# Where tiles begin in a partition of SBUF: two layers of a decoder trunk on one core, with operands of TensorE moved by 32 to 512 bytes

## The chip, the core and the metric

The kernel runs on one core of a Trainium2 chip. Times are device microseconds of one execution. The engines are PE (TensorE: matmuls, and PEld for the loading of their weights), DVE (VectorE), ACT (ScalarE), POOL (GpSimd) and SP, which here only issues DMAs. SBUF is the core's memory of 128 partitions; "a tile begins at byte b" means the byte within each partition. What is measured is the median time of the whole launch.

## The reference, cut to what matters

Two layers over 512 tokens of 1024 columns. Each layer adds, in this order, a half-step SwiGLU feed-forward net (FFN), a token mixer (differential attention in layer 0, causal pooling in layer 1), a cross attention with 4 heads into 256 memory tokens, and a second FFN; after each comes a layer norm. All in float32.

```
for i in range(DEPTH):                                   # DEPTH = 2
    x = layer_norm(a*x + 0.5*swiglu_ffn(x, w_in[i,0], w_out[i,0]))      # 1024 -> 2*2816 -> 1024
    h = diff_attention(x, ...) if i == 0 else pool_mixer(x, ...)
    x = layer_norm(a*x + h)
    x = layer_norm(a*x + memory_cross_attention(x, mem, wq[i], wkv[i], wo[i]))
    x = layer_norm(a*x + 0.5*swiglu_ffn(x, w_in[i,1], w_out[i,1]))
```

## The kernel before

Every float32 product is made of three matmuls: each operand is split into a rounded part (hi, made by a cast on ACT) and the rest (lo, made by a subtraction on DVE), and `mm3` issues hi·hi, hi·lo and lo·hi. So wh and wl are the two parts of a weight tile, xh and xl those of the transposed activations. A matmul names a stationary operand, 128 columns of it, loaded by an LDWEIGHTS of its own, and a moving operand of 256 or 512 columns. Which of the two a "weight" of the network is depends on the stage: in the FFN's first half and the query projections x moves and the weight is loaded; in the FFN's second half (`down`, `plain_down`) and the output projections (`to_tokens`) the weights move and the activations (ha, hb, xe, oT) are loaded.

The FFN's first half uses a seven-product scheme (`up`) with moving operands of 256 columns; 7,392 of the 13,104 matmuls stand there. Its second half has moving operands of 512 columns. The differential attention (DA) projects q and k with 512 columns, v with 256; the cross attention projects q with 512 (for some parts 256) and the memory's k and v with 256.

SBUF is laid out by pools that are opened one behind the other. `stage_pools` opens the pools of weights of a stage (wh, wl, and the raw float32 they are split from), `phase_pool` those of a phase. A tile's place follows from the order of the pools and their sizes; `pad` opens an idle pool of some bytes so that what follows begins elsewhere. `APART` is 64, `ROUND` is 512. Sizes of nearly all tiles are multiples of 512 bytes, so what a pad sets holds until the next pad. Pools of different stages lie over one another: a tile of a later stage that covers a byte of a tile of an earlier one has to wait until that one is read for the last time, whatever the number of bytes.

The output projection of DA (`to_tokens` at the end of `diff_attention`) keeps the split weights of its last half in tiles that are free by then: `low, low, p, p`. The cross attention of layer 0 begins beside it: `load_memory("p")` loads the 256 memory tokens into four tiles p (four DMAs on SP's queue, which is strictly in order), transposes them on PE (line 1175) and splits them into mem0h, mem0l and so on; `xa_kv` then splits its first weights (lines 237 and 239) and multiplies them with the memory (pk, pv). The layer norm between them works token block by token block (X_74 to X_77 are the four blocks): `ln_add` (line 352) adds the projection, `ln_token` computes the mean (361), the variance (ACT line 374, POOL lines 375 and 376) and scales (378, 380).

The order of instructions on each engine is set when the program is built, by the tile framework's scheduler, from its dependences; each engine then runs its own list strictly in order and waits at semaphores.

Of the kernel before, what the change touches and what calls it, by code (L numbers as in the profile page):

```python
# [9 lines left out]
F32 = mybir.dt.float32  # L10
# [7 lines left out]
P = 128  # L18
# [33 lines left out]
APART, ROUND, LINE = 64, 512, 480  # L52
# [52 lines left out]
class Trunk:  # L105
# [31 lines left out]
            pool = ctx.enter_context(self.pool("pad"))  # L137
            pool.tile([P, nbytes // 4], F32, tag="pad", name="pad")

    def to_x(self, ctx):  # L140

        self.pad(ctx, ROUND - APART)

    def to_w(self, ctx):

        self.pad(ctx, APART)

    @contextmanager
    def phase_pool(self, gain, spare, **bufs):

        self.gain, self.spare, self.bufs, self.phase = gain, spare, bufs, {}
        with ExitStack() as ctx:
            for t in bufs:
                if t == "_x":
                    self.to_x(ctx)
                else:
                    self.phase[t] = ctx.enter_context(self.pool(t))
            yield  # L160

    @contextmanager
    def stage_pools(self, w, raw, order):

        with ExitStack() as ctx:
            self.stage = {}
            for n in order:
                if n == "wl" and order[0] == "mem" or n == "wh" == order[0]:
                    self.to_w(ctx)
                self.stage[n] = ctx.enter_context(self.pool(n))  # L170
            self.banks = {n: ctx.enter_context(self.pool(n, space=PSUM)) for n in ("px", "py", "yz")}
            self.w_bufs, self.raw_bufs, self.aux_turn = w, raw, 0
            yield
# [982 lines left out]
    def load_memory(self, tag=None):  # L1156

        nc = self.nc
        src = self.a["mem"][0].rearrange("(m p) (h d) -> p m h d", p=P, h=2)
        if tag:  # L1160
            raw = [[self.tmp(tag) for h in range(2)] for m in range(2)]
            for m in range(2):
                for h in range(2):
                    nc.sync.dma_start(raw[m][h], src[:, m, h])
        else:
            t = self.raw_tile((2, 2, S))
            nc.sync.dma_start(t, src)
            raw = [[t[:, m, h] for h in range(2)] for m in range(2)]
        self.memT = []
        for c in range(0, KC, 2):  # L1170
            pt = self.aux("pt").rearrange("p (c m n) -> p c m n", c=2, m=2)
            for i in range(2):
                for m in range(2):
                    o = (c + i) % 4 * P
                    self.nc.tensor.transpose(pt[:, i, m], raw[m][c // 4][:, o : o + P], self.ident)
            t = tuple(self.stage["mem"].tile([P, 2, MEM], F32R, name=f"mem{c}{n}") for n in "hl")
            self.split(t[0], t[1], pt.rearrange("p c m n -> p c (m n)"))
            self.memT += [(t[0][:, i], t[1][:, i]) for i in range(2)]
        if tag and LINE < 480:
            self.stage["mem"].tile([P, (480 - LINE) // 4], F32, name="mempad")  # L1180

    def xa_kv(self, w, h):
        nc = self.nc
# [102 lines left out]
            yield from self.xa_head(*self.heads[h][1])  # L1286

    def cross_attention(self, layer, ln):
        bufs = dict(q=8, oT=10, gb=2)
        if layer == 0:  # L1290
            self.kv = []
            mem = self.side_pool("mem")
            with self.other_pools():
                self.stage["mem"] = mem
                with self.phase_pool(("gb", "gb"), "p", pT=6, p=4, kv=8, _x=0, **bufs):
                    self.kvp = self.phase["kv"]
                    with self.tc.high_priority():
                        self.load_memory("p")
                    self.xa(layer, ln)
            self.close_side()  # L1300
        else:
            with self.later, self.phase_pool(("gb", "gb"), "p", _x=0, pT=6, p=4, **bufs):
                self.xa(layer, ln)

    def xa(self, layer, ln):
# [44 lines left out]
        self.side.pop().__exit__(None, None, None)  # L1350

    def ffn_pools(self):
        return self.stage_pools(4, dict(ra=4, rc=3), ("wh", "wl", "ra", "rc"))

    def other_pools(self, order=("wh", "wl", "raw")):
        return self.stage_pools(5, dict(raw=2), order)

    def ffn_phase(self, **more):
        bufs = dict(b1=1, b3=1, b2=1, b4=1, _x=0, xe=6, hb=4, sp=4, ha=4, sr=1, hr=3)
        return self.phase_pool(("hr", "sr"), "sp", **bufs, **more)  # L1360

    def ffn_first(self, layer, ln):
# [13 lines left out]

    def mixer(self, layer, ln):
        if layer == 0:
            bufs = dict(low=4, rt=2, a=4, p=4, o=1, qk=8, _x=0, v=4, oT=11)
            with self.other_pools(), self.phase_pool(("v", "v"), "rt", **bufs):  # L1380
                self.diff_attention(layer, ln)
            self.close_side()
        else:
            self.later = ExitStack()
            self.later.enter_context(self.other_pools(("mem", "wl", "raw", "wh")))
            self.kvp = self.later.enter_context(self.pool("kv"))
            bufs = dict(pw=1, pb=2, ps=2, ones=1, _x=0, pooled=20, sq=1)
            with self.phase_pool(("pooled", "pooled"), "sq", **bufs):
                side = self.pool_mixer(layer, ln)
                with self.tc.high_priority():  # L1390
                    self.load_memory()
                next(side)
                self.kv = []
                self.weave(self.early_kv(layer, 2), side, 900, 4300)
            self.close_side()
# [45 lines left out]
```

## Time and profile before

| | |
|---|---|
| runs | median 1972.75 us of three, 1970.02 to 1975.78 |
| the profiled execution | 1976.36 us, of which the profile's span is 1974.6 us |
| PE busy | 97% of the span, 13,104 matmuls, and as many weight loads |
| DVE, ACT, POOL busy | 79%, 51%, 16% |
| granted clock of TensorE, mean | 0.995 |

Matmuls are pipelined: a row's duration is longer than the distance from one start to the next. What a stream of matmuls costs is therefore read from starts: the start of the first and of the last of a run of equal ones, divided by the number of steps between them. The view by line gives the duration of one; it goes up and down with that distance, but is not it.

### The profile page before, as it was taken

What the parts mean: (1) busy time and instruction counts of PE and PEld (TensorE: products, weight loads), DVE (VectorE), ACT (ScalarE), POOL (GpSimd) and SP (SyncE); (2) the same over time, 40 slices, a digit from 0 to 9 for tenths busy, and PEclk for the clock granted to TensorE, in tenths of its full rate; (3) what the DMA queues carried; (4) which work ended last, traced back from release to release, by engine and by line L of the source; (5) the groups of instructions that cost most, each with busy time, mean ns of one, the idle gap of its engine ahead of it and who ended that gap; (6) DMA issues with size and microseconds to landing.
All of it is one profiled execution on the core that took longest, in us unless ns stands there. A gap on an engine that the chain in (4) does not pass through costs nothing. (4 is left out here: it accounts for less than half of the span.)

```text
span 1974.6 us, 32506 instructions
## 1 busy us (share of the span) xinstructions
PE 1920.2 (97%) x13104; PEld 1749.0 (89%) x13104; DVE 1566.1 (79%) x2208; ACT 1016.0 (51%) x1545; POOL 320.1 (16%) x297
## 2 busy tenths in 40 slices
PE   7999999999999999999999999999999999999998
PEld 7999998888778888999998999999788889899996
DVE  7888987888867558789887888888777457888886
ACT  5554553466655435555553655555445435555552
POOL 1122121111211002221220311211100013111211
PEclk9999999999999999999999999999989999999999
DMA  9988772322134316977783787877254336877861
GB/s 238 197 171 181 166 156 64 89 65 86 45 116 139 108 65 160 203 176 166 145 193 112 149 176 168 181 171 139 77 171 131 104 96 143 168 173 170 184 143 46
DMA packets 246743, 277.96 MB, mean 141 GB/s; under 512 B 8256, under 2 KB 212544, under 8 KB 246592
## 3 DMA queue, kind: packets, MB, share of 16 engines
q0 software_dynamic: 92928, 92.29, 30.3%
q1 hardware_dynamic: 153664, 183.59, 28.8%
q8 instruction: 103, 1.69, 0.3%
q14 instruction: 48, 0.39, 0.1%
HBM read 273.75 MB, written 2.10 MB: 140 GB/s over the span
## 5 line engine op out<-in xcount | busy, mean ns | idle before, releaser
L578 POOL DMA_DIRECT2D ra<-in_ffn_w_in_dram x132 | 171.4, 1316 | 1017.0 <-DVE wl L115 850.9
L114 ACT CAST wh<-ra 128x1024 fp32r<-128x1024 f32 x184 | 192.9, 1053 | 218.1 <-DMA ra<-in_ffn_w_in_dram 55.7
L115 DVE TENSOR_TENSOR wl<-ra,wh 128x1024 fp32r<-128x1024 f32 x184 | 223.6, 1221 | 82.1 <-ACT wh L114 81.4
L114 ACT CAST wh<-rc 128x1024 fp32r<-128x1024 f32 x136 | 142.7, 1053 | 129.3 <-PE x L198 39.2
L197 PE MATMUL x<-xh,wh 128*128 128x256 f32 x704 | 197.5, 281 | 6.3 <-DVE hr L644 4.1
L197 PE MATMUL x<-xe,wh 128*128 128x256 f32 x704 | 195.3, 277 | 3.1 <-ACT sp L639 1.7
L198 PE MATMUL x<-xl,wh 128*128 128x256 f32 x704 | 196.5, 279 | 1.5 <-DVE xl L115 1.5
L199 PE MATMUL x<-xh,wl 128*128 128x256 f32 x704 | 196.1, 279 | 0.8 <-DVE wl L115 0.8
L198 PE MATMUL x<-xe,wh 128*128 128x256 f32 x704 | 194.8, 277 | 0.0
L199 PE MATMUL x<-xe,wl 128*128 128x256 f32 x704 | 194.7, 277 | 0.0
L115 DVE TENSOR_TENSOR wl<-rc,wh 128x1024 fp32r<-128x1024 f32 x136 | 164.6, 1220 | 27.5 <-ACT wh L114 27.1
L114 ACT CAST wh<-b 128x1024 fp32r<-128x1024 f32 x112 | 117.7, 1051 | 125.7 <-PE x L198 62.0
L115 DVE TENSOR_TENSOR wl<-b,wh 128x1024 fp32r<-128x1024 f32 x112 | 136.8, 1222 | 41.0 <-ACT wh L114 41.0
L197 PEld LDWEIGHTS x<-xh,wh 128*128 128x128 f32 x704 | 133.2, 189 | 9.4 <-issue 4.4
L197 PEld LDWEIGHTS x<-xe,wh 128*128 128x128 f32 x704 | 132.2, 188 | 5.0 <-ACT ha L639 1.9
L198 PEld LDWEIGHTS x<-xl,wh 128*128 128x128 f32 x704 | 133.4, 189 | 3.3 <-DVE xl L115 2.1
L199 PEld LDWEIGHTS x<-xh,wl 128*128 128x128 f32 x704 | 133.2, 189 | 1.0 <-DVE wl L115 1.0
L198 PEld LDWEIGHTS x<-xe,wh 128*128 128x128 f32 x704 | 132.3, 188 | 1.3
L199 PEld LDWEIGHTS x<-xe,wl 128*128 128x128 f32 x704 | 132.4, 188 | 0.0
L115 DVE TENSOR_TENSOR wl<-raw,wh 128x1024 fp32r<-128x1024 f32 x64 | 80.5, 1264 | 56.1 <-ACT wh L114 55.4
L114 ACT CAST wh<-raw 128x1024 fp32r<-128x1024 f32 x64 | 66.6, 1051 | 71.5 <-PE xq L198 22.7
L199 PE MATMUL z<-xh,wl 128*128 128x256 f32 x352 | 97.9, 280 | 4.0 <-DVE wl L115 4.0
(413 smaller groups left out, 6156.5 us busy)
## 6 DMA issues: line engine op xcount, KB each, us to landing
ra<-in_ffn_w_in_dram POOLq DMA_DIRECT2D x132, 512.0 KB, 7.2
rc<-in_ffn_w_in_dram SPq DMA_DIRECT2D x88, 512.0 KB, 6.0
b<-in_ffn_w_out_dram SPq DMA_DIRECT2D x76, 512.0 KB, 5.7
ra<-in_ffn_w_in_dram SPq DMA_DIRECT2D x44, 512.0 KB, 4.7
rc<-in_ffn_w_in_dram POOLq DMA_DIRECT2D x44, 512.0 KB, 9.8
raw<-in_xa_wkv_dram SPq DMA_DIRECT2D x16, 1024.0 KB, 5.3
raw<-in_da_w_qkv_dram SPq DMA_DIRECT2D x16, 512.0 KB, 5.2
raw<-in_xa_wq_dram SPq DMA_DIRECT2D x8, 1024.0 KB, 5.1
```

Of the source, the lines that this page charges most:

```text
L114: self.nc.scalar.copy(hi, src),
L115: self.nc.vector.tensor_sub(lo, src, hi.bitcast(F32)),
L197: mm(out, w[0], x[0], start=start, stop=False, skip_group_check=again)
L198: mm(out, w[0], x[1], start=False, stop=False, skip_group_check=again)
L199: self.last_mm = mm(out, w[1], x[0], start=False, stop=stop, skip_group_check=again)
L578: nc.gpsimd.dma_start(t, source(*block), accum_op=ALU.add)
```

## The change

The two functions that padded at fixed places give way to one, `step`, and a list of pools can name a pad wherever it likes: `_off` is 64 bytes, `_32` and `_96` are 32 and 96, any other (`_on`, `_on_gb`) is 448. The pads are then set anew in each stage. No operation, no tile and no size is added or removed apart from the pads, and the strip at the end of the memory's pool.

```
+    def step(self, ctx, name):
+        given = {"_off": APART, "_32": 32, "_96": 96}
+        self.pad(ctx, given.get(name, ROUND - APART))
...
-                if n == "wl" and order[0] == "mem" or n == "wh" == order[0]:
-                    self.to_w(ctx)
-                self.stage[n] = ctx.enter_context(self.pool(n))
+                if n[0] == "_":
+                    self.step(ctx, n)
+                else:
+                    self.stage[n] = ctx.enter_context(self.pool(n))
...
-        if tag and LINE < 480:
-            self.stage["mem"].tile([P, (480 - LINE) // 4], F32, name="mempad")
+        if tag:
+            self.stage["mem"].tile([P, (ROUND - APART) // 4], F32, name="strip")
...
-        bufs = dict(q=8, oT=10, gb=2)
+        bufs = dict(_off=0, q=8, _on=0, oT=10, _on_gb=0, gb=2)
...
-            with self.other_pools():
+            with self.other_pools(("_32", "wh", "wl", "raw")):
...
-                with self.phase_pool(("gb", "gb"), "p", pT=6, p=4, kv=8, _x=0, **bufs):
+                with self.phase_pool(("gb", "gb"), "p", pT=6, p=4, kv=8, **bufs):
...
-            with self.later, self.phase_pool(("gb", "gb"), "p", _x=0, pT=6, p=4, **bufs):
+            with self.later, self.phase_pool(("gb", "gb"), "p", pT=6, p=4, **bufs):
...
-        return self.stage_pools(4, dict(ra=4, rc=3), ("wh", "wl", "ra", "rc"))
+        return self.stage_pools(4, dict(ra=4, rc=3), ("_off", "wh", "wl", "ra", "rc"))
...
-        bufs = dict(b1=1, b3=1, b2=1, b4=1, _x=0, xe=6, hb=4, sp=4, ha=4, sr=1, hr=3)
+        bufs = dict(b1=1, b3=1, b2=1, b4=1, _on=0, xe=6, _off=0, hb=4, sp=4, ha=4, sr=1, hr=3)
...
-            bufs = dict(low=4, rt=2, a=4, p=4, o=1, qk=8, _x=0, v=4, oT=11)
+            bufs = dict(low=4, rt=2, a=4, p=4, o=1, qk=8, v=4, oT=11)
...
-            self.later.enter_context(self.other_pools(("mem", "wl", "raw", "wh")))
+            self.later.enter_context(self.other_pools(("mem", "_96", "wl", "raw", "wh")))
...
-            bufs = dict(pw=1, pb=2, ps=2, ones=1, _x=0, pooled=20, sq=1)
+            bufs = dict(pw=1, pb=2, ps=2, ones=1, _off=0, pooled=20, sq=1)
```

Where tiles begin, as the remainder of their first byte by 512, before and after:

| stage | tiles | before | after |
|---|---|---|---|
| all | xh, xl | 480 | 480 |
| FFN | wh, wl / xe / ha, hb | 32 / 480 / 480 | 32 / 480 / 32 |
| DA | wh, wl, low, a, p, qk / v, oT | 32 / 480 | 480 / 480 |
| cross attention, layer 0 | wh, wl, pT, p, kv / mem / q / oT | 32 / 480 / 480 / 480 | 0 / 32 / 64 / 0 |
| pooling and cross attention, layer 1 | wh, wl, kv / pT, p / mem / q / oT | 32 / 480 / 480 / 480 / 480 | 64 / 64 / 480 / 128 / 64 |

While a matmul streams its moving operand, PE loads the weights of the next one. The *distance* in what follows is the start of a matmul's moving operand less the start of the next matmul's weights, by 512, written between -255 and 256. Counted over the list of matmuls, float32 ones that are followed by another such:

| columns | distance before | after | matmuls |
|---|---|---|---|
| 256 | -64 | -64 | 7,272 |
| 256 | 64 | 0 / -64 / -32 / 96 | 354 / 266 / 189 / 188 |
| 256 | -64 | -96 / 32 / 0 | 279 / 187 / 80 |
| 512 | 64 | 0 | 1,667 |
| 512 | -64 | 0 | 406 |
| 512 | 0 | 64 | 376 |
| 512 | -64 | -32 / -96 | 189 / 139 |
| 512 | 64 | 64 | 289 |
| 512 | 0 | 0 | 195 |

One more thing follows from the places. Before, the stages DA and cross attention of layer 0 begin with the same pad, and the four tiles p of the cross attention lie exactly on the four tiles a of DA (bytes 137,760 to 145,952). After, DA has no pad and the cross attention one of 32 bytes: DA's a lies at 137,696 to 145,888 and its p from 145,888 on; the cross attention's p at 137,728 to 145,920, so that the last of them covers 32 bytes of DA's first p.

The order of instructions is the same on every engine except at this one boundary, on DVE, ACT, PE and SP (and two loads for a layer norm of layer 1 that change places on SP). On DVE, before, from the addition for the third token block's end to the third weight split (X_76 and X_77 are the last two token blocks, mem0l to mem6l the low parts of the transposed memory, wl those of the first weights of `xa_kv`):

```order
L352 SCALAR_TENSOR_TENSOR X_77,sums<-X_77,ps 128x512
L378 SCALAR_TENSOR_TENSOR X_76<-X_76,mean,v 128x1024
L115 TENSOR_TENSOR mem4l<-pt,mem4h 128x512
L380 SCALAR_TENSOR_TENSOR X_76<-X_76,rstd,v 128x1024
L115 TENSOR_TENSOR xl<-pt,xh 128x4x128 x2
L352 SCALAR_TENSOR_TENSOR X_77,sums<-X_77,ps 128x512
L115 TENSOR_TENSOR mem0l<-pt,mem0h 128x512
L115 TENSOR_TENSOR mem2l<-pt,mem2h 128x512
L115 TENSOR_TENSOR mem6l<-pt,mem6h 128x512
L361 TENSOR_SCALAR mean<-sums 128x1
L239 TENSOR_TENSOR wl<-raw,wh 128x1024
```

And the same place of the change (its line numbers are two lower):

```order
L350 SCALAR_TENSOR_TENSOR X_77,sums<-X_77,ps 128x512
L376 SCALAR_TENSOR_TENSOR X_76<-X_76,mean,v 128x1024
L115 TENSOR_TENSOR xl<-pt,xh 128x4x128
L378 SCALAR_TENSOR_TENSOR X_76<-X_76,rstd,v 128x1024
L115 TENSOR_TENSOR xl<-pt,xh 128x4x128
L350 SCALAR_TENSOR_TENSOR X_77,sums<-X_77,ps 128x512
L359 TENSOR_SCALAR mean<-sums 128x1
L376 SCALAR_TENSOR_TENSOR X_77<-X_77,mean,v 128x1024
L378 SCALAR_TENSOR_TENSOR X_77<-X_77,rstd,v 128x1024
L237 TENSOR_TENSOR wl<-raw,wh 128x1024 x2
L115 TENSOR_TENSOR mem0l<-pt,mem0h 128x512
```

The whole scaling of the last token block and two weight splits now stand ahead of mem0l, where before mem0l followed the addition at once. On ACT, in the same way, the last block's square (`rt,var<-X_77,mean`) now stands ahead of the casts of wh and mem0h. On PE, before, from the last two products of DA's output projection on:

```order
L199 MATMUL ps<-p,oT 128x512
L1175 MATMUL pt<-ident,p 128x128 x12
L197 MATMUL pk<-mem0h,wh 128x256
L197 MATMUL pv<-wh,mem0h 128x256
L198 MATMUL pk<-mem0l,wh 128x256
```

And of the change:

```order
L197 MATMUL ps<-p,oT 128x512
L1173 MATMUL pt<-ident,p 128x128 x16
L195 MATMUL pk<-mem0h,wh 128x256
L196 MATMUL pk<-mem0l,wh 128x256
```

All sixteen transposes of the memory now stand behind the projection, where four of them stood within it, and the product with mem0l is PE's second one after them. On SP the four loads of p stand where they stood, but the second of them now waits for a product of DA's output projection that reads p, and the loads behind it in SP's queue wait with it.

More of the change, by code (lines that the diff above doesn't have):

```diff
@@ L138, in pad @@
             pool.tile([P, nbytes // 4], F32, tag="pad", name="pad")
[L140 to L146, printed above, removed]
+    def step(self, ctx, name):
+        given = {"_off": APART, "_32": 32, "_96": 96}
+        self.pad(ctx, given.get(name, ROUND - APART))
     @contextmanager
@@ L155, in phase_pool @@
             for t in bufs:
-                if t == "_x":
-                    self.to_x(ctx)
+                if t[0] == "_":
+                    self.step(ctx, t)
                 else:
```

## The prediction

> **What bounds the kernel now.** I read the page first, then the order of time on PE.
>
> ```profile
> span 1974.6 us, 32506 instructions
> PE 1920.2 (97%) x13104; PEld 1749.0 (89%) x13104; DVE 1566.1 (79%) x2208; ACT 1016.0 (51%) x1545; POOL 320.1 (16%) x297
> ```
>
> PE is busy for 97% of the span, so the time is the sum of the distances between matmul starts, plus the few places where PE stands. The change touches both: how fast a stream of matmuls runs, and one place where PE may stand. For the first, the timeline of PE, start in us and duration; of each run the first and the last start:
>
> ```profile
> 620.04 0.40 PE L197 MATMUL xq<-xh,wh 128*128 128x512 f32 x1
> ...
> 625.64 0.40 PE L197 MATMUL xq<-xh,wh 128*128 128x512 f32 x1
> ...
> 104.29 0.39 PE L197 MATMUL pz<-wh,hb 128*128 128x512 f32 x1
> ...
> 107.04 0.28 PE L197 MATMUL z<-xe,wh 128*128 128x256 f32 x1
> ...
> 322.50 0.39 PE L197 MATMUL ps<-hb,xe 128*128 128x512 f32 x1
> ...
> 324.12 0.39 PE L198 MATMUL ps<-hb,xe 128*128 128x512 f32 x1
> ...
> 325.25 0.39 PE L197 MATMUL ps<-ha,xe 128*128 128x512 f32 x1
> ...
> 330.69 0.40 PE L197 MATMUL ps<-wh,xe 128*128 128x512 f32 x1
> ```
>
> All have 512 columns, and nothing waits within a run. At distance -64 (x at 480, weights at 32) 24 steps take 5.60 us, 233.3 ns each. At 64 (weights moving, hb loaded) 12 steps take 2.75, 229.2 each. At 0 (hb and ha moving, xe loaded) 24 steps take 5.44, 226.7 each, though the 7 steps from 322.50 to 324.12 took 231.4. So the distance is worth 2.5 and 6.6 ns per matmul, and a stream may for a while run 4 to 5 ns slower whatever the distance. For 256 columns:
>
> ```profile
> 1660.02 0.28 PE L197 MATMUL z<-xh,wh 128*128 128x256 f32 x1
> ...
> 1662.29 0.28 PE L199 MATMUL z<-xh,wl 128*128 128x256 f32 x1
> ...
> 1199.72 0.28 PE L198 MATMUL x<-xe,wh 128*128 128x256 f32 x1
> ...
> 1201.25 0.28 PE L199 MATMUL x<-xe,wl 128*128 128x256 f32 x1
> ```
>
> Both are at -64: 20 steps in 2.27 us (113.5 ns) and 13 in 1.53 (117.7 ns). Here there are two paces at one and the same distance; the slow one comes and goes.
>
> **The change, part by part.** No instruction is added or removed; the sum has three terms.
>
> *First, PE stands at the boundary from DA to the cross attention.* The rows of before there, by engine:
>
> ```profile
> 601.63 0.39 PE L199 MATMUL ps<-p,oT 128*128 128x512 f32 x1
> 604.75 0.39 PE L198 MATMUL pk<-mem0l,wh 128*128 128x256 f32 x1
> ...
> 602.21 1.28 DVE L115 TENSOR_TENSOR xl<-pt,xh 128x512 fp32r<-128x512 f32 x2
> 603.40 0.68 DVE L352 SCALAR_TENSOR_TENSOR X<-X,ps 128x512 f32<-128x512 f32 x1
> 604.01 0.68 DVE L115 TENSOR_TENSOR mem0l<-pt,mem0h 128x512 fp32r<-128x512 f32 x1
> 606.06 0.20 DVE L361 TENSOR_SCALAR mean<-sums 128x1 f32<-128x1 f32 x1
> 606.18 1.22 DVE L239 TENSOR_TENSOR wl<-raw,wh 128x1024 fp32r<-128x1024 f32 x1
> 607.32 1.22 DVE L115 TENSOR_TENSOR wl<-raw,wh 128x1024 fp32r<-128x1024 f32 x1
> 608.45 1.28 DVE L378 SCALAR_TENSOR_TENSOR X<-X,mean,v 128x1024 f32<-128x1024 f32 x1
> ...
> 606.36 1.15 ACT L374 ACTIVATE rt<-X,mean 128x1024 bf16<-128x1024 f32 x1 [1.05 <-DVE mean L361]
> 607.69 0.89 POOL L375 TENSOR_SCALAR var<-var 128x1 f32<-128x1 f32 x1 [6.80 <-ACT rt L374]
> 608.67 1.46 POOL L376 TENSOR_TENSOR rstd<-var,mhalf 128x1 f32<-128x1 f32 x1
> ...
> p<-in_mem_dram SPq DMA_DIRECT2D x4, 256.0 KB, 3.3
> ```
>
> Before, mem0l follows the last addition at once and PE's product with it starts at 604.75. Afterwards the last token block's whole scaling and two splits stand ahead of mem0l on DVE. The addition itself starts about 0.6 us earlier, at 602.8, since one xl split (half of the 1.28) now stands further ahead. From its start: to the mean 0.7 and the mean 0.2; the square on ACT from 606.36 to POOL's start at 607.69, 1.33; POOL's two steps from 607.69 to 610.13, 2.44; X by rstd, two splits at 1.13 each from start to start, and mem0l: 1.2, 2.3, 0.7. That is 8.9 us, so PE's product starts near 611.7, 6.9 us later than before. Beside it: ACT comes to mem0h after the square and two casts, some 4 us earlier than that; the loads of p, now held back until a product of the last group on p (which ends near 601), land 3.3 us after their issue, and the sixteen transposes end near 605.5. Both are covered by DVE's chain; without it, p would still cost about 1 us. Behind the held p on SP wait a load of weights and the layer norm's gains, which land before DVE and ACT get to them. Little of what PE did meanwhile is saved: one product with wh. I take +6.8, between 5 and 8.
>
> *Second, the clock.* PE then has nearly nothing to do from 605.5 to 611.7. The rows of the nearest such place, and of the other one at which the granted clock fell; the columns after the stretch are PE, PEld, DVE, ACT and POOL busy, and further on the granted clock:
>
> ```profile
> 37.25 0.39 PE L199 MATMUL z<-xh,wl 128*128 128x256 f32 x1 [3.37 <-DVE wl L115]
> ...
> 38.40:41.70 3.30, 3.30 (x18) 3.30 (x17) 3.30 (x6) 0.45 (x1) 3.17 (x3) 0.50 0.47 70
> 41.80:45.20 3.40, 3.40 (x32) 3.40 (x31) 3.40 (x5) 2.09 (x4) 0.15 (x1) 1.00 1.22 193
> ...
> 1444.70:1458.20 13.50, 13.50 (x66) 13.50 (x65) 10.71 (x15) 8.53 (x12) 0.00 (x0) 0.50 0.38 118
> 1458.30:1461.70 3.40, 3.40 (x31) 3.40 (x31) 2.03 (x3) 1.64 (x4) 0.00 (x0) 1.00 0.33 108
> ```
>
> After 3.4 idle us the clock was halved for 3.3 us, in which 18 matmuls ran, where 32 run in the 3.4 us behind it: 13 lost, at 113.5 ns 1.5 us. I take +1.5, between 0 (it falls while PE stands) and 6.3 (as in the second place: 66 matmuls in 13.5 us, where 31 in 3.4 make 123; 57 times 0.11).
>
> *Third, the pace.* By the counts of the table of distances: 512 columns from -64 to 0, 406 times 6.6 ns, 2.7 us; from 64 to 0, 1,667 times 2.5, 4.2 us; from 0 to 64, 376 times -2.5, -0.9 us. The 328 from -64 to -32 and -96 have no row: between 226.7 and 233.3, the two that lie around -32, so 3.3 each, 1.1 us, with 0 and 2.2 as ends, and 2.2 of loss if -96 lies as far beyond 233.3. That is 7.1 us. Of it I count two thirds, 4.8: the run from 322.50 shows that distance 0 goes at 231.4 as well, and where DVE or DMA is late next PE waits for them instead. The 1,543 of 256 columns that move go to 0, to 64 of the other sign, to 32 and to 96. At 64 of the one sign there are the paces 113.5 and 117.7, so nothing for the sign; for the others I take nothing too, with 4.2 ns either way as ends.
>
> Sum: 6.8 + 1.5 - 4.8 = +3.5 us. Against the profiled execution's 1976.36 that is 1979.9; against the median of the runs, 3.6 below it, 1976.3, which I predict: 0.18% more, within the 0.3% that a measurement of this kernel can hardly tell from no change (its three runs lie 0.29% apart).
>
> A rule speaks against the third term. The Trainium skill, in "TensorE: Matmul & The Clock Gate", under "Step-by-step: what each phase is for", says that PE has two independent read ports into SBUF, and that loading the next weights takes no read bandwidth from the running matmul. By it places would not matter, and the sum would be its first two terms alone. The rows of 226.7 and 233.3 do not agree with it.
>
> **The rivals.**
>
> *The places do not matter to the pace.* Then the 6.6 ns come from the work around it (the run at 620 has DMA beside it, that at 325 none), and +8.3 remains: 1981.0, slower by 0.42%. This is where the skill's rule leads. Against it: the run at 104 stands amid loads as well and goes at 229.2.
>
> *The new distances cost at 256 columns.* 1,277 matmuls (the 1,543 less the 266 from 64 to -64) go to 0, 32 and 96, of either sign, none of which has a run here. If they take the slow pace throughout, that is 1,277 times 4.2, 5.4 us: +8.9, 1981.6. It decides from 2.4 us on, 1.9 ns for each. For it: the products of DA's values and of the memory, which move, stand among scores and transposes, where the slow pace comes often. Against it: nothing at 64 depends on the sign.
>
> *The clock stays low for long*, as at 1444: 4.8 more than taken, +8.3, 1981.1. For it: transposes and short waits lie around the place. Against it: what follows the wait is a dense run of products with the memory, as at 38.4, where it recovered at once.
>
> *The slow pace goes away.* If a stream at distance 0 also ends in the fast pace, the 256-column streams behind the FFN's second half start fast. A stretch at 117.7 gives back 3.6% of its length. With the third of the pace that I left out (2.4) it takes 7.0 us more to be faster by over 0.3%, 195 us of slow stretches that turn fast; with all of them the time would be about 1966.5. For it: DA and the stretch about 1200 are slow. Against it: DA's boundary stall stays, and the slow pace at 1199 stands at a distance that the change leaves alone.
>
> **How the numbers follow.** The forecast has a chance of 0.46, all of it within 0.3%. Places without effect 0.13, dear distances 0.19, a low clock 0.10: together 0.42, slower by over 0.3% (beyond 1978.7). The slow pace gone: 0.12, faster (below 1966.8). The forecast's own range is 1971 to 1980, from the ends of the stall (2 us down, 1 up) and of the pace (2.4 down, and 2 up). To hold eight in ten it reaches to the slower cases with 4 us for their own scatter, 1985, and to 1968 below.
>
> **What would show it.** Right: on PE, a wait of 4 us or more for DVE's mem0l at the start of the cross attention, and the second load of p issued near 601; DVE's list there as in the order; a row of half clock behind it; runs of `pz<-wh,hb` near 226.7 to 228 and of DA's q and k near 227 to 229; the FFN's 256-column runs unchanged at 113.5. Wrong: no wait there; 512-column runs at 0 still at 229 to 233; `pk` and `pv` above 118; or a longer wait at another boundary, where the places changed but the order did not.

## The result, and the profile after

The changed kernel takes 1999.66 us (median of five, 1993.7 to 2001.5) against 1973.47 us (five, 1970.02 to 1975.78): the ratio is 1.0128, 95% interval 1.0109 to 1.0147. Forecast was 1976.3, between 1968 and 1985. It is 1.3% slower, 23 us above the forecast and 15 above its range. Both kernels run at half clock in a few stretches, whose length differs from one execution to the next: the change's five had a mean granted clock of 0.992 to 0.994 and took 2001.5 to 1993.7 us.

The page of the changed kernel begins so:

```profile
span 1999.7 us, 32505 instructions
PE 1940.6 (97%) x13104; PEld 1772.8 (89%) x13104; DVE 1566.7 (78%) x2208; ACT 1015.3 (51%) x1545; POOL 320.7 (16%) x297
```

Against before, PE's busy time has grown by 20.4 us of the span's 25.1, with the same number of matmuls, and that of DVE, ACT and POOL by less than 1 us. So the larger part is no wait: PE works on the same list and takes longer over it. Where, the timeline of PE shows, here a 512-column run of the FFN's second half and the 256-column run behind it (start in us, duration; the first and the last of each, and the first of the next):

```profile
104.97 0.39 PE L195 MATMUL pz<-wh,hb 128*128 128x512 f32 x1
...
107.46 0.39 PE L197 MATMUL pz<-wh,hb 128*128 128x512 f32 x1
107.69 0.28 PE L195 MATMUL z<-xe,wh 128*128 128x256 f32 x1
...
113.22 0.28 PE L197 MATMUL z<-xe,wl 128*128 128x256 f32 x1
113.34 0.39 PE L195 MATMUL pz<-wh,hb 128*128 128x512 f32 x1
```

The twelve of 512 columns take 2.72 us, 226.7 ns each, as forecast for distance 0. The 48 of 256 columns behind them take 5.65 us, 117.7 ns each, at a distance of -64 that the change leaves alone. In the kernel before, the same run began at 107.04 and ended where the next pz began:

```profile
112.50 0.39 PE L197 MATMUL pz<-wh,hb 128*128 128x512 f32 x1
```

That is 5.46 us, 113.8 each: the first five at 117.7, the rest at 113.3. In the changed kernel all 48 go at 117.7, and so it is behind nearly every 512-column run of the four FFN stages.

The other part stands at the boundary from DA to the cross attention. The timeline of SP, DVE and PE there, and behind it two windows (columns: length, then PE, PEld, DVE, ACT and POOL busy, then the granted clock, the share of DMA and GB/s):

```profile
604.92 1.28 SPq L1162 DMA_DIRECT2D p<-in_mem_dram  x3
...
608.45 0.21 DVE L359 TENSOR_SCALAR mean<-sums 128x1 f32<-128x1 f32 x1
610.03 1.28 DVE L376 SCALAR_TENSOR_TENSOR X<-X,mean,v 128x1024 f32<-128x1024 f32 x1 [1.37 <-ACT rt L372]
612.02 1.29 DVE L378 SCALAR_TENSOR_TENSOR X<-X,rstd,v 128x1024 f32<-128x1024 f32 x1 [0.71 <-POOL rstd L374]
613.22 2.36 DVE L237 TENSOR_TENSOR wl<-raw,wh 128x1024 fp32r<-128x1024 f32 x2
615.49 0.69 DVE L115 TENSOR_TENSOR mem0l<-pt,mem0h 128x512 fp32r<-128x512 f32 x1
...
616.24 0.58 PE L196 MATMUL pk<-mem0l,wh 128*128 128x256 f32 x1 [2.99 <-DVE mem0l L115]
```

```profile
608.40:622.00 13.60, 9.10 (x41) 8.36 (x41) 10.21 (x14) 8.61 (x12) 1.82 (x2) 0.50 0.65 232
622.10:625.50 3.40, 3.40 (x32) 3.40 (x31) 1.78 (x2) 0.72 (x2) 0.00 (x0) 1.00 0.95 285
```

PE's product with mem0l starts at 616.24, 11.49 us later than in the kernel before. By its starts PE was 4.9 us behind already when it came to this boundary, so the boundary itself makes this product 6.6 us later, through the chain forecast: mean, scaling, two splits of weights, mem0l. The clock is halved from 608.4 to 622.0, over four times as long as taken.

The whole difference, added up from the starts of the two profiled executions (a matmul counts from its start to the next start):

| what | us |
|---|---|
| 7,272 matmuls of 256 columns whose distance stays -64: mean 114.20 to 116.58 ns where nothing waits | +17.1 |
| the other matmuls of 256 columns, nearly all with a new distance | +4.2 |
| all matmuls of 512 columns | -4.65 |
| waits, transposes and half clock, nearly all at the boundary | +8.4 |
| sum | +25.05 |

### The profile page after: what moved, and what is told of

The parts are those of the page before. It is cut to its first block, busy times and chain, and to the rows that moved or that the text cites. A ratio compares the mean times of both kernels' runs of the same rounds, so it can differ in the third digit from the quotient of the medians.

```text
span 1999.7 us, 32505 instructions
## 1 busy us (share of the span) xinstructions
PE 1940.6 (97%) x13104; PEld 1772.8 (89%) x13104; DVE 1566.7 (78%) x2208; ACT 1015.3 (51%) x1545; POOL 320.7 (16%) x297
## 5 line engine op out<-in xcount | busy, mean ns | idle before, releaser
L195 PE MATMUL x<-xe,wh 128*128 128x256 f32 x704 | 197.3, 280 | 2.5 <-ACT sp L637 1.6
L196 PE MATMUL x<-xe,wh 128*128 128x256 f32 x704 | 197.1, 280 | 0.0
L114 ACT CAST wh<-b 128x1024 fp32r<-128x1024 f32 x112 | 117.8, 1052 | 133.3 <-PE x L196 65.4
L197 PE MATMUL y<-xh,wl 128*128 128x256 f32 x352 | 99.5, 283 | 2.2 <-DVE wl L115 2.2
```

The costliest lines, as they stand in the source:

```text
L114: self.nc.scalar.copy(hi, src),
L195: mm(out, w[0], x[0], start=start, stop=False, skip_group_check=again)
L196: mm(out, w[0], x[1], start=False, stop=False, skip_group_check=again)
L197: self.last_mm = mm(out, w[1], x[0], start=False, stop=stop, skip_group_check=again)
```

## The experiments

Two theories stood against each other at first. A: a run of 512 columns at distance 0 hands a slow pace on to the run of 256 columns behind it. B: the slow pace comes from some other part of the change. Distances and paces below are read as above, from the starts.

**One part alone.** Of the tiles that PE reads only hb and ha move, in the kernel before:

```
     for t in bufs:
-        if t == "_x":
-            self.to_x(ctx)
+        if t[0] == "_":
+            (self.to_w if t[1] == "w" else self.to_x)(ctx)
...
-    bufs = dict(b1=1, b3=1, b2=1, b4=1, _x=0, xe=6, hb=4, sp=4, ha=4, sr=1, hr=3)
+    bufs = dict(b1=1, b3=1, b2=1, b4=1, _x=0, xe=6, _w=0, hb=4, sp=4, ha=4, sr=1, hr=3)
```

> The kernel before, with hb and ha alone moved to byte 32, so that the 512-column runs of the FFN's second half stand at distance 0 and everything else where it was. Theory A (a run of 512 columns at distance 0 hands the slow pace on to the run of 256 columns behind it): the FFN's 256-column runs at 117.7 ns instead of 113.8, the 512-column runs at 226.7 instead of 228.8; the four FFN stages of the change lost 17.5 us and won 2.9 by this, so +14.6 us, about 1988. Rival B (the slow pace comes from the other places that the change moves, or from the long stall at the boundary): only the 2.9 us are won, 1970.6, and 256 columns stay at 113.8.

Measured: 1987.07 us against 1973.88, ratio 1.0067 (1.0052 to 1.0082). On PE:

```profile
129.86 0.39 PE L197 MATMUL px<-wh,hb 128*128 128x512 f32 x1
...
132.58 0.28 PE L197 MATMUL x<-xh,wh 128*128 128x256 f32 x1
...
138.23 0.39 PE L197 MATMUL px<-wh,hb 128*128 128x512 f32 x1
```

Twelve steps of 226.7 ns, then 48 of 117.7. This pad alone makes the kernel 13.2 us slower: theory A. Matched one by one with the kernel before, the FFN's 256-column matmuls lose 17.6 us in the profiled execution (17.1 in the change), and those of 512 win 2.9. The boundary is as before here.

**The reverse**, the change without that pad (`_off=0` ahead of hb taken out of `ffn_phase`):

> The change without its pad ahead of hb and ha, so that the 512-column runs of the FFN's second half are at distance 64 again. Theory A: the 256-column runs of the FFN go back to about 113.8 ns, -14.6 us against the change, about 1985. Rival B (another part of the change causes the slow pace): they stay at 117.7 and 2.9 us are lost on the 512-column runs, about 2002.5.

Measured: 1985.45 us, 14.2 below the change, as expected. The FFN's 256-column matmuls have a mean of 114.4 again. Not all runs recover, though. In one early stretch:

```profile
129.46 0.40 PE L195 MATMUL px<-wh,hb 128*128 128x512 f32 x1
...
132.22 0.28 PE L195 MATMUL x<-xh,wh 128*128 128x256 f32 x1
...
137.88 0.40 PE L195 MATMUL px<-wh,hb 128*128 128x512 f32 x1
```

At distance 64 the 512 columns go at 230.0 here, and the 48 behind them at 117.9 throughout. So at 64 there are two ways through: entered at 113.3, the run of 512 goes at 229 and the next 256 columns recover after five; entered at 117.7, it goes at 230 to 231 and nothing recovers. In both, a run at 64 passes on the pace in which it was entered.

**Only part of the runs.** In the kernel before, ha is moved ahead of hb and a pad of 64 put between them:

```
-    bufs = dict(b1=1, b3=1, b2=1, b4=1, _x=0, xe=6, hb=4, sp=4, ha=4, sr=1, hr=3)
+    bufs = dict(b1=1, b3=1, b2=1, b4=1, _x=0, xe=6, ha=4, _w=0, hb=4, sp=4, sr=1, hr=3)
```

> The kernel before, with hb alone at byte 32 and ha left at 480: of the 512-column runs of the FFN's second half those with hb (pz) are at distance 0, those with ha (px) at 64. Theory A: the 256-column runs behind a pz run go at 117.7 ns throughout, those behind a px run start so and go at 113.3 after some five matmuls; the time rises by about half of 14.6, 7.3 us, to 1981. Rival C (the new place of the tiles disturbs PE through what other engines write there or read, whatever ran before): the 256-column runs behind both kinds are slow alike, in proportion to the moved tiles, a mean near 115.7 behind either; the time is about the same, so the split by run decides.

Measured: 1986.55 us against 1973.88, ratio 1.0066 (1.0051 to 1.0081). The expectation was wrong in two ways. Five of the seven runs of a turn use hb, not half, and the first of the two with ha is no cure:

```profile
146.09 0.40 PE L197 MATMUL px<-wh,ha 128*128 128x512 f32 x1
...
148.85 0.28 PE L197 MATMUL y<-xh,wh 128*128 128x256 f32 x1
...
149.44 0.28 PE L199 MATMUL y<-xh,wl 128*128 128x256 f32 x1
```

This run at distance 64 is entered at 117.7, goes at 230.0 and leaves at 118, so it shows the same passing on as the stretch above. Neither theory A as first written nor C says that. The pace falls to 113.3 only behind the next run of this kind, py. One product of py stands ahead of the others, in the middle of the y run (at 151.92). Behind it y goes on at 118 ns; then come the rest of py, and z:

```profile
154.88 0.40 PE L198 MATMUL py<-wl,ha 128*128 128x512 f32 x1
...
157.44 0.28 PE L197 MATMUL z<-xh,wh 128*128 128x256 f32 x1
```

The eleven of py, at 64 and entered at 117.7 like px, go at 233, and z goes at 113.3 from its fourth matmul on. Seven runs of this kernel do so. So at 64 there is a third way through, and the pace at the entry does not settle by itself which one a run takes. What the single product changes is not shown.

**The boundary.** DA's `bufs` of the change get 512 bytes of pad between a and p:

```
-            bufs = dict(low=4, rt=2, a=4, p=4, o=1, qk=8, v=4, oT=11)
+            bufs = dict(low=4, rt=2, a=4, _off=0, _on=0, p=4, o=1, qk=8, v=4, oT=11)
```

> The change with 512 bytes of pad more between a and p of DA: no distance differs from the change, but the cross attention's p no longer covers a byte of DA's first p, and DVE's list has mem0l right behind the last addition again, as before the change. If the 32 shared bytes cause the stall of 6.7 us and the half clock of 13.65 us that begins in it: PE's product with mem0l starts within 2 us of the projection's end, no half clock near 610, and the time is 9 to 11 us below the change, 1989 to 1991. Rival D (the memory's loads, or DVE's backlog at the boundary, hold PE all the same): a stall of 4 us or more stays, and at most 4 us are won, 1996 or more.

Measured: 1991.61 us, 8.05 below the change. The timeline of DVE and PE in this kernel, and a window:

```profile
608.24 0.68 DVE L350 SCALAR_TENSOR_TENSOR X<-X,ps 128x512 f32<-128x512 f32 x1
...
608.85 0.68 DVE L115 TENSOR_TENSOR mem0l<-pt,mem0h 128x512 fp32r<-128x512 f32 x1
...
611.14 0.58 PE L195 MATMUL pk<-mem0h,wh 128*128 128x256 f32 x1 [1.89 <-ACT wh L235]
```

```profile
610.80:617.50 6.70, 5.89 (x26) 5.60 (x27) 6.12 (x7) 4.36 (x6) 2.69 (x2) 0.50 0.44 144
```

mem0l follows the addition at once. From the start of the projection's last product to the product with mem0l pass 4.87 us, where it was 10.82 in the change and 3.12 before. So the 32 shared bytes make most of the stall. A half clock of 6.7 us stays, against the expectation, and ACT's cast of the weights still makes PE wait for 1.89 us.

Not all of the 8.05 us comes from here. By the starts from the 3,800th to the 4,100th matmul, this profiled execution is 4.3 us shorter than that of the change. Another 5.7 us lie in the pooling stage, where the pad alters neither order nor distances. There the half clock lasted half as long; a window of the change and one of this kernel (length, PE busy, granted clock, share of DMA, GB/s):

```profile
1465.30:1478.80 13.50, 13.50 (x65) 0.50 0.37 118
...
1450.50:1457.10 6.60, 5.93 (x28) 0.50 1.07 338
```

Its length there differs between kernels that are alike in that stage: 13.7 us before, 6.8 with hb and ha moved alone, 3.4 with hb alone. What the boundary itself gives back is therefore put at 4.3 us.

**Both repairs**, taken together in the change:

> The change with both repairs: no pad ahead of hb and ha, and 512 bytes more between a and p of DA. If the two causes are apart, the two savings add: from 1999.7 by 14.2 and by 8.05 to about 1977.4, and what is left over the kernel before, some 3.5 us, lies in the cross attentions' 256-column streams at distances 0, 32 and 96. Rival L (the same microseconds were counted in both): 1981 or more.

Measured: 1979.06 us against 1972.63, ratio 1.0034 (1.0022 to 1.0046). The savings add to within 2 us, and rival L's 1981 isn't reached; with half clocks of different length this says little about the boundary. 6.4 us remain over the kernel before. By the starts of the profiled execution the boundary still costs 5.3 (from the 3,800th to the 4,100th matmul), and the 256-column matmuls outside the FFN's first half, nearly all at new distances, 3.5, as expected; those of 512 win 1.5, and the pooling stage, with 6.8 us of half clock, is 5.9 shorter than in the profiled execution of the kernel before, which had 13.7.

**Other distances.** Is 0 special, or 64? In the kernel before, hb and ha go to byte 0 (a pad of 32 ahead of hb), so the runs of 512 stand at 32:

> The kernel before with hb and ha at byte 0: the 512-column runs of the FFN's second half at distance 32, 256 columns at -64 as before. Theory G (a run of 512 columns hands on the slow pace only where it streams undisturbed at 226.7 ns, and any distance but 0 disturbs it): 512 columns above 228 ns, the 256-column runs behind them five slow matmuls and then 113.3, the time within 3 us of the kernel before. Rival H (64 is special, every other distance acts like 0): 512 columns at 226.7 and the 256-column runs at 117.8, about 1987.

Measured: 1995.94 us against 1976.58, ratio 1.0084 (1.0051 to 1.0117). Both were wrong, it is worse than either:

```profile
130.16 0.39 PE L197 MATMUL px<-wh,hb 128*128 128x512 f32 x1
...
132.96 0.28 PE L197 MATMUL x<-xh,wh 128*128 128x256 f32 x1
...
138.62 0.39 PE L197 MATMUL px<-wh,hb 128*128 128x512 f32 x1
```

512 columns at 233.3, and 256 behind them at 117.9. So the slow pace isn't handed on because the run before streams without disturbance.

Then hb and ha at byte 224 (a pad of 256), so that the runs of 512 stand at -192:

> The same with hb and ha at byte 224, the 512-column runs at distance -192. Theory G: as before the change, within 3 us of it (or slower, if the 512-column runs go at 233 as at -64: 1,232 times 4.2, 5 us more). Rival H: 1987, 256 columns at 117.8.

Measured: 1975.37 us against 1976.58, ratio 0.9995 (0.9982 to 1.0008). Its runs go at 228.8 or 230.9 ns and hand on 113.3 or 117.7, number for number like those at 64, which is 256 bytes from -192. That the distance counts by 256 bytes, not 512, was not in either theory.

Next the distance of the 256 columns themselves. wh, wl, hb and ha begin at 96 (pads of 128, 384 and 128 ahead of wh, xe and hb):

> The FFN with wh, wl, hb and ha at byte 96 and xe at 480: 512 columns at distance 0 as in the change, 256 columns at -128 in place of -64. Theory E (the slow pace is there at any distance and only the run before decides): 256 columns at 117.8, about 1987 as with hb and ha moved alone. Theory F (the slow pace belongs to a distance of 64): 256 columns at 113.3 throughout, where the kernel before has a mean of 114.2 over 7,272 of them, and 512 at 226.7: 6.3 and 2.9 us won, 1965.

Measured: 2003.86 us against 1976.58, ratio 1.0138 (1.0098 to 1.0177):

```profile
130.68 0.39 PE L200 MATMUL px<-wh,hb 128*128 128x512 f32 x1
...
133.45 0.28 PE L200 MATMUL x<-xh,wh 128*128 128x256 f32 x1
...
139.20 0.39 PE L200 MATMUL px<-wh,hb 128*128 128x512 f32 x1
```

At -128 the 256 columns go at 119.8, and the 512 columns at distance 0 go at 230.8 here, not at 226.7: the run before matters to them too. With wh, wl, hb and ha at 224 the 256 columns stand at 256:

> The same with wh, wl, hb and ha at byte 224: 512 columns at distance 0, 256 columns at 256, as far apart as they can be. Theory E: 256 columns at 117.8, about 1987. Theory F: 256 columns at 113.3 throughout, 1965.

Measured: 1998.57 us, ratio 1.0111 (1.0074 to 1.0148); 119.9 ns, which is also what the changed kernel's 256 columns at distance 0 come near (119.2). Theory F is out: of the three distances only -64 has the pace of 113.3, and the other two are worse throughout. Theory E's 117.8 is missed as well.

**Without any 512-column run.** If nothing of 512 columns is there, nothing should hand the slow pace on. In `product` of the kernel before, the loop over k is put in one over two halves of the columns:

```
+            for n in (0, 256):
+                n = slice(n, n + 256)
                 for k in range(2):
                     h, l = hs[k][a]
-                    self.mm3(ps, (h[:, o], l[:, o]), ws[k], start and k == 0, k == 1, not start)
+                    x = (ws[k][0][:, n], ws[k][1][:, n])
+                    first = start and k == 0 and n.start == 0
+                    self.mm3(ps[:, n], (h[:, o], l[:, o]), x, first, k == 1, not start or n.start > 0)
```

> The kernel before, with each 512-column matmul of the FFN's seven-product second half issued as two of 256 columns (the left half of the product, then the right half); the places are those of before, so the new ones are at distance 64 and all of the FFN's runs have 256 columns. Theory I (256 columns have the paces 113.3 and 117.7 at 64 as at -64, and without a 512-column run nothing hands over the slow one): the former 512 columns take 226.7 in place of 228.8 ns (about 1,000 times 2.1, 2.1 us won) and the five slow matmuls behind each of 84 runs go (84 times 5 times 4.4, 1.8 us): 4 us below the kernel before, near 1970. Rival J (the change from moving activations to moving weights is itself what starts the slow pace): the 256-column runs stay slow on both sides of each change, 17 us or more above it, 1990.

Measured: 1983.68 us against 1972.63, ratio 1.006 (1.0047 to 1.0074), between the times of theory I and of rival J.

```profile
104.49 0.28 PE L197 MATMUL pz<-wh,hb 128*128 128x256 f32 x1
...
107.21 0.28 PE L197 MATMUL z<-xe,wh 128*128 128x256 f32 x1
...
112.87 0.28 PE L197 MATMUL pz<-wh,hb 128*128 128x256 f32 x1
...
115.70 0.28 PE L197 MATMUL x<-xe,wh 128*128 128x256 f32 x1
...
121.15 0.28 PE L197 MATMUL px<-wh,hb 128*128 128x256 f32 x1
```

The paces from run to run are 113.3, 117.9, 117.9, 113.5. A run of 24 at 64 that goes at 113.3 is followed by one of 48 at 117.9, and one that goes at 117.9 by one at 113.5, in 90 of the 96 places. So a pace of 113.3 at 64 isn't the same thing as one of 113.3 at -64. With every 512-column product of a full tile halved:

> The kernel before, with every float32 matmul of 512 columns whose product fills a whole 128 by 512 tile issued as two of 256 columns, in the attention stages too. Theory I: the streams at distance -64 win most (734 times 6.5 ns, 4.8 us), those at 64 in the attention about 2 us, beside the 4 us of the FFN: near 1963. Rival K (behind the waits of the attention stages the slow pace holds, and two matmuls of 117.7 cost more than the 231 of one of 512): about 1,700 times 4.5 ns lost there, so 1970 or above, no better than with the FFN's alone.

Measured: 2002.64 us, ratio 1.0147 (1.0126 to 1.0168): rival K's side, and by more than it said. At 0 the halves of the products that move hb, ha (in the FFN's last quarter) and q go at 119.8 (two make 239.6; one of 512 takes 228.5 in the kernel before), and at 64 the halves go at 116.3. Some of the loss is a half clock of 30.7 us in the pooling stage of its profile.

With the halves and hb and ha at 96, so that all of the FFN's runs stand at -64:

> The kernel with the halved matmuls of the FFN's second half, and hb and ha at byte 96, so that its 256-column runs stand at distance -64 like those of the first half. Theory M (there are two phases; at -64 one of them goes at 113.3 and the other at 117.7, at 64 it is the other way round, and a run hands its phase on): no run changes sides any more, nearly all of the FFN's matmuls go at 113.3 ns, where with the halves at 64 one of each two neighbouring runs went at 117.8. Against the kernel before 4 us are won as with theory I, and some 282 of 512 columns in its last quarter, at 128 instead of 0, lose 1 us: near 1970, 14 us below the halves at 64. Rival N (each change between moving weights and moving activations turns the pace over, whatever the distance): as with the halves at 64, about 1984.

Measured: 1984.62 us against 1973.08, ratio 1.0053 (1.0035 to 1.0072). Theory M falls: nearly every run of 24 goes at 117.5 (2.82 us) and nearly every one of 48 between them at 114.0, all through the FFN. The pace changes over at both ends of the short runs, as rival N says, though with the halves at 64 it did so at one end only. None of the three versions with halves beats the kernel before.

**Streams alone.** Last, a kernel of nothing but such runs on one tile, with DVE and ACT at work only between the blocks:

```
+    def run256(self, d, n):          # X moves, W is loaded, X begins d bytes behind W
+        x0 = (32 + d) % 512 // 4
+        for i in range(n):
+            w = self.T[:, 2056 + i % 8 * 128 : 2184 + i % 8 * 128]
+            m = self.T[:, x0 + i % 4 * 256 : x0 + i % 4 * 256 + 256]
+            self.mm(self.ps[:, :256], w, m)
+
+    def run512(self, d, n):          # W moves, H is loaded, W begins d bytes behind H
+        h0 = 5120 + (32 - d) % 512 // 4
+        for i in range(n):
+            w = self.T[:, h0 + i % 8 * 128 : h0 + i % 8 * 128 + 128]
+            m = self.T[:, 2056 + i % 4 * 512 : 2568 + i % 4 * 512]
+            self.mm(self.ps, w, m)
...
```

> Nothing but runs of matmuls on one loaded tile, no other engine at work beside them, so nothing of the reference is computed and its time compares with nothing. First part, for each distance d of 0, 32 and so on to 480: 36 matmuls of 256 columns at -64, 12 of 512 at d, 36 of 256 at -64, 12 of 512 at 0, 12 of 256 at -64, 12 of 512 at d, 36 of 256 at -64. Second part: 256 columns at each d around a run of 512 at 64 and one at 0. Third part: 256 columns at -64 with activations moving in turn with 256 columns with weights moving at 64, -64, 0 and 128. Theory O (the places and the run before decide, other engines have no part): 512 columns near 226.7 ns at 0 and 256, 228.8 or 230.9 at 64 and 320, 232 to 234 at the others; 256 columns at 113.3 or 117.7 at 64, 192, 320 and 448 and at 117 to 120 elsewhere; behind 512 at 0 all 256-column matmuls at -64 at 117.7, behind 512 at 64 five of them and then 113.3 if the run of 512 was entered at 113.3; in the third part the paces change over at each change of kind. Rival P (traffic of the other engines makes the slow pace): 113.3 and 226.7 at all distances and behind all runs.

Measured, in a single execution at a granted clock of 1.0, in the order of time, one row for a stretch within one run, from two blocks (the second column is the busy time of all N in the row; the pace is that, less 0.28 or 0.39 for the last one's own, by N-1; all have the same line and names). First a block of the second part, 256 columns at -64 around a run of 512 at 64 and one at 0:

```profile
686.26 1.86 PE L94 MATMUL ps<-T 128*128 128x256 f32 x15
...
688.08 2.45 PE L94 MATMUL ps<-T 128*128 128x512 f32 x10
...
691.42 3.56 PE L94 MATMUL ps<-T 128*128 128x256 f32 x30
...
695.40 2.21 PE L94 MATMUL ps<-T 128*128 128x512 f32 x9
...
698.02 3.93 PE L94 MATMUL ps<-T 128*128 128x256 f32 x32
```

113 ns; 512 columns at 64, 229; 113.1 behind them; 512 columns at 0, 227; 117.7 behind them. And a block of the first part, with 512 columns at 96:

```profile
110.98 3.34 PE L94 MATMUL ps<-T 128*128 128x256 f32 x27
...
114.27 2.75 PE L94 MATMUL ps<-T 128*128 128x512 f32 x11
...
117.66 3.56 PE L94 MATMUL ps<-T 128*128 128x256 f32 x30
```

Here the run of 512 is entered at 117.7, goes at 236 (234.9 from its fourth matmul on), and what follows goes at 113.1: at 96, a run cures the slow pace. A window of the first block, with DVE, ACT and POOL as the third to fifth of the busy times, and behind the clock the share of DMA and GB/s:

```profile
690.90:694.90 4.00, 4.00 (x37) 4.00 (x36) 0.00 (x0) 0.00 (x0) 0.00 (x0) 1.00 0.02 4
```

DVE, ACT and POOL did nothing while these ran, and DMA next to nothing, so rival P is out. The places and what ran before decide, theory O. In its third part, runs of 256 columns that move weights stand between those at -64 that move activations. With the weights' distance at 64 the pace changes at one end of such a run, at -64 from the second run on at both ends, as in the two kernels with halves. At 0 and 128 the runs at -64 between them stay at 113.3, so the change of kind alone does not turn the pace over, against the expectation. The table gives what each distance does, without the first three steps of a run; distances that are 256 bytes apart gave the same paces to within 1.3 ns and are put together. "Hands on" is the pace of 256 columns at -64 behind a run of 512, by the pace before it ("?" was not seen).

| distance, by 256 | 512 columns, ns | entered at 113.3, hands on | entered at 117.8, hands on | 256 columns, ns |
|---|---|---|---|---|
| 0 | 226.6 to 230.6 | 117.8 | 117.8 | 119.6 to 120.1 |
| 32 | 233.3 | 117.8 | 117.8 | 116.7 |
| 64 | 228.5 to 229.6 | 113.3, after some five | 117.8 | 113.4 or 117.8 |
| 96 | 234.9 | ? | 113.3 | 119.9 |
| 128 | 232.0 | 117.8 | 113.3 | 118.6 to 120.0 |
| 160 | 234.0 | 117.8 | 117.8 | 118.7 |
| 192 (-64) | 233.4 | 117.8 | 113.3 | 113.3 or 117.8 |
| 224 | 233.2 | 113.3 | 117.8 | 118.3 |

## Why the prediction was wrong, step by step

**The stall at the boundary: right.** +6.8 was taken for PE's product with mem0l, between 5 and 8; it came 6.6 us later, by the steps forecast. The kernel with DA's p moved aside shows that the 32 bytes cause most of it. The loads of p behind the first were issued at 604.92, that is at 600.0 less the 4.9 us by which PE was behind, where near 601 was forecast. The transposes ended some 2 us later than forecast, so the wait for mem0l itself is 2.99 us and not 4 or more; DVE covered this, as argued.

**The clock: the size was off.** +1.5 was taken, from the place where the clock recovered after 3.3 us; it stayed low for 13.6, as at the other place, which the text had as a rival. Half of that lay in the wait, where it cost little. Of the 5.8 us from 616.24 to 622.0 about half is lost, 2.7. Stall and clock together made the stretch around the boundary (from the 3,800th matmul to the 4,100th) 9.3 us longer, where 8.3 were counted.

**The pace of 512 columns: right in the sum, by luck in part.** -4.8 was counted, -4.65 measured, and the FFN's runs at 0 go at 226.7 where the forecast read 226.7. But DA's q and k, counted to fall by 6.6 ns, fell from 233.0 to 229.7. The cross attentions' xq, counted to win 3.3, went from 233.4 to 233.6. The third that was left out, for another reason, happens to be about as much. The rival that places do not matter is out: in the streams alone the same 512 columns take 226.6 or 234.9 ns by their distance. The Trainium skill ("TensorE: Matmul & The Clock Gate", "Step-by-step: what each phase is for") says that loading the next weights takes no read bandwidth from the running matmul. What the prediction drew from it, that places would not matter, does not hold here; whether the two read ports share anything is not shown.

**The pace of 256 columns: wrong, and this decided.** The step was the sentence that takes nothing for 256 columns, and the last section's "the FFN's 256-column runs unchanged at 113.5". In its place stand +17.1 us on matmuls whose distance the change leaves alone and +4.2 on the others. The second is the rival of dear new distances, which had a chance of 0.19 and a price of 5.4. For the first there was no case with that sign. The rival that lets the slow pace go away had the mechanism, a run of 512 columns that settles the pace of the run behind it, but it took for granted that a stream at distance 0, which goes fast itself, leaves the fast pace behind. It is the other way round, as the kernel with hb and ha alone moved shows (+13.2 us).

The trace of before had the answer, in rows that the prediction does not show. The last quarter of each FFN streams at distance 0 there, and a later FFN begins behind one of these runs:

```profile
1098.90 0.39 PE L199 MATMUL ps<-ha,xe 128*128 128x512 f32 x1
1099.13 0.28 PE L197 MATMUL x<-xh,wh 128*128 128x256 f32 x1
...
1101.84 0.28 PE L199 MATMUL x<-xh,wl 128*128 128x256 f32 x1
```

The 23 steps behind it take 2.71 us, 117.8 ns each, without the recovery after five that follows nearly every run at 64. In the kernel with hb and ha alone moved, the same eighteen products ahead, which move hb and ha, stand at 64, and there the run behind them recovers:

```profile
1107.89 0.28 PE L197 MATMUL x<-xh,wh 128*128 128x256 f32 x1
...
1108.49 0.28 PE L199 MATMUL x<-xh,wl 128*128 128x256 f32 x1
...
1110.53 0.28 PE L199 MATMUL x<-xh,wl 128*128 128x256 f32 x1
```

Five steps take 0.60 us, the eighteen behind them 2.04, 113.3 ns each. So the pad that makes the runs elsewhere slow makes this one fast. It is so in all eight profiles that have the eighteen at 0 (or 256) or at 64.

The prediction saw that the slow pace "comes and goes" and priced it as scatter. A pace that lasts for hundreds of matmuls and sits on 7,272 of them should have been traced to where it begins and ends before anything was costed beside it: 4 ns on them are 29 us, more than all terms of the sum together.

**What stays open.** The runs show which paces there are, and what hands them on. They do not show what in the hardware the two paces are, nor why 256 bytes is the period. Where hb and ha move, the last matmul ahead of each FFN run, which moves x, changes its distance too (from 0 to -64, as hb is loaded next), and in the streams the two go together. At 1098.90 transposes stand ahead of the eighteen in both kernels and the hand-on turns all the same, so a run's own distance is the likelier cause, but no run here was made to part the two. Nor is that distance all of it: with hb and ha at byte 0 the runs at 32 leave 117.8 in the FFN, and the eighteen at 32 leave 113.3. The start of a load against the start of the matmul before it is the same 3 ns in both paces in the trace. A run of 512 at 0 with its last matmuls at 96 might take the gain without the loss, by the table; it was not tried, and its 2 or 3 us are less than a measurement here can tell.

## What to carry to other kernels

Before pricing an edit that makes one stream of matmuls faster, read the pace of the stream behind it: here a run that gains 25 ns in twelve matmuls makes the next 48 lose about 190. Where a trace shows two paces for the same instruction at the same operands, find what stands ahead of each change from one to the other, and count how many instructions it would reach. And when tiles move by a few bytes, list which old tile each new one covers: 32 bytes of overlap held PE up for 6 us more and cost 4.3 at that boundary.

## What the runs showed of the hardware that was not expected

- Matmuls of float32 parts have a pace that depends on the distance between the moving operand and the next weights, by 256 bytes: 226.6 to 234.9 ns for 512 columns and 113.3 to 120.1 for 256, with PE alone at work.
- At one and the same distance (-64) 256 columns have two paces, 113.3 and 117.8; a pace that has settled goes on as long as nothing interrupts it. A run of 512 columns between them keeps the pace, sets it, or turns it over, mostly by its own distance: at 0 it leaves 117.8 wherever nothing waits, at 96 it left 113.3.
- Splitting a matmul of 512 columns into two of 256 costs nothing by itself at 113.3, but at 64 and -64 the change between the two kinds of operand turned the pace over: 11 us lost in the two kernels that did it in the FFN alone.
- The clock was at half for 13.6 us at a boundary where PE waited, with transposes and one product between the waits, and went on at half for 5.8 us of dense products.
